# Mean squares of x by TensorE from the turned x, and bias rows on 64 partitions, in one step of a hybrid streaming encoder

## The chip, the cores and the metric

One NeuronCore of a Trainium2 chip runs the whole program in one launch. The metric is the device time of one execution in microseconds (us); three runs of the kernel before took 1779.07, 1780.92 and 1783.11 us, and their median is 1780.92 us. All data is float32. The engines are TensorE (PE), VectorE (DVE), ScalarE (ACT), GpSimd (POOL) and SyncE (SP), which issues the DMA transfers here.

## The reference

One layer of an encoder is computed for a prompt of 1024 rows and a sample of 64 rows; together they are 1088 rows of width 1024. What matters here is the first part, the normalised projection into queries, keys, values and forget logits:

```
def rms_norm(x, g):
    y = x * rsqrt(mean(x * x, axis=-1) + EPS)
    return y * g

h = rms_norm(x, g_norm1)
p = h @ w_in            # q_A k_A v_A | q_B k_B v_B | forget logits
```

Behind it come chunk-band attention with a learned relative-position bias (8 heads), forgetting attention (8 heads), an output projection, cross-attention into 256 memory tokens, and a feed-forward block with a causal convolution. The bias of the chunk-band attention depends on the distance of query and key alone: bias[i, j] = table[clip(i - j, -128, 128) + 128].

## The kernel before

The gain g_norm1 is multiplied into x ahead of the projection, and the factor rsqrt(mean + EPS) of each row is applied behind it. So the projection needs x turned (features on the partitions, rows along the free axis), and the mean square of each row has to be known when the products leave PSUM. The host hands over both forms: xT, turned, and xn, row by row.

The projection is done for eight pairs of heads, p = 0 to 7. Each pair goes through eight row tiles of 128 rows, t = 0 to 7, and one tile of the 64 sample rows. Pair 0 is also the stage in which x is loaded. Turned x comes in column chunks c = 0 to 4: chunks 0 to 3 hold 256 rows each, which are row tiles 2c and 2c + 1, and chunk 4 holds the samples. Each chunk is loaded in two halves z of four feature blocks k (load_x, line 163). split_x (line 126) makes two parts of each block: xhi on ACT (line 130; on POOL, line 128, for odd k of chunk 0) and the rest xlo on DVE (line 131). Each row tile's product (line 299) is then three matmuls for each of eight k, into a PSUM bank "pj".

The mean squares are done from xn: load_stats (line 144) loads 128 rows by 1024 into a tile "s", stats (line 149) squares them on ACT with a sum along the row into one column of ssq, and stats_end (line 156) adds EPS and forms rstd1 and eps1 with Ln, Exp and a refining step (rsq, line 72). proj (line 303) reads the product: ACT copies it (qkraw, line 309), squares it for the norm of queries and keys (line 233) and scales the values by rstd1 (line 312). Then norm does the norm of queries and keys on DVE and POOL, and turn transposes them on PE (line 326, bank "tq", of which there is one) and has ACT and DVE write kh, kl and q (lines 265 and 266). Scores (line 499), softmax (lines 502 to 509), transposes (line 539) and sums (line 554) of the attention are sub-steps too.

Order: weave (line 274) puts sub-steps between the pieces of three matmuls of a row tile's product. After piece number x + 1 of n, it issues sub-steps as long as the number issued times n is below the number of sub-steps times (x + 1); so the first sub-step comes right behind the first piece. early (line 591) says which loading work of pair 0 goes in front of (first list) or behind (second list) the other sub-steps of tile t. Row tiles 0 and 1 are done together, as 16 pieces that alternate between them. Everything is traced in this order; a scheduler may then change the order of an engine's instructions by when it thinks that they are ready. in_order (line 1822) keeps it from that: up to the end of t = 5 of pair 0, each instruction of PE, ACT, DVE and POOL is tied behind the one traced before it on its engine, and SP's up to load_rows(0) at the end of the opening. Later only a few kinds are tied.

The bias: load_rows (line 181) copies a head's row of the table, 769 long, to 128 rows in DRAM, and load_bias (line 445) reads them with a step of 768, which shifts each row by one (toeplitz, line 439); the lower 64 partitions read the copies 64 to 127. The samples' attention reads 64 such rows.

Of the kernel before, what the change touches and what calls it, by code (L numbers as in the profile page):

```python
# [7 lines left out]
F32 = mybir.dt.float32  # L8
F32R = mybir.dt.float32r
ACT = mybir.ActivationFunctionType  # L10
# [31 lines left out]
def hybrid_step(ctx: ExitStack, tc: tile.TileContext, i: dict, o: dict):  # L42
# [24 lines left out]
    sv = dram.tile([8, S, P], F32, name="sv")  # L67
    rows = dram.tile([8, P, 769], F32, name="rows")
    negc = dram.tile([8, T], F32, name="negc")
    negs = dram.tile([8, N], F32, name="negs")  # L70

    def rsq(pl, ms, out, n, rows=P):

        y = pl.tile([rows, n], F32, name="rsq_y", bufs=3)
        a = pl.tile([rows, n], F32, name="rsq_a", bufs=3)
        act.activation(y, ms, ACT.Ln)
# [8 lines left out]
    eps1 = small.tile([P, 9], F32, name="eps1")  # L85
    ssq = small.tile([P, 9], F32, name="ssq")
    flog = small.tile([P, 9, 8], F32, name="flog")
# [3 lines left out]
    dve.memset(flog, 0.0)  # L91
    dve.memset(ssq, 1.0)

# [47 lines left out]

    xns = {}

    def load_stats(t):
        rows = P if t < NT else S
        xn = xns[t] = wk.tile([P, N], F32, name="s", bufs=4)
        nc.sync.dma_start(xn[:rows, :D], i["xn"][t * P:t * P + rows])

    def stats(t):
        rows = P if t < NT else S  # L150
        if t not in xns:
            load_stats(t)
        xn = xns.pop(t)
        act.activation(xn[:rows, :D], xn[:rows, :D], ACT.Square, scale=1.0 / 32, accum_out=ssq[:rows, t:t + 1])

    def stats_end(t0, t1):
        ms = wk.tile([P, 9], F32, name="ms1", bufs=2)
        n = t1 - t0
        dve.tensor_scalar(ms[:, :n], ssq[:, t0:t1], EPS, None, op0=ALU.add)
        rsq(wk, ms[:, :n], rstd1[:, t0:t1], n)  # L160
        dve.tensor_scalar(eps1[:, t0:t1], ms[:, :n], EPS, None, op0=ALU.mult)

# [14 lines left out]
    def columns(c, z, raw=None):  # L177
        raw = raw or load_x(c, z)
        return [lambda k=k: split_col(c, k, raw) for k in range(4 * z, 4 * z + 4)]

    def load_rows(p):
        for head in range(2 * p, 2 * p + 2):
            nc.sync.dma_start(rows[head], i["table"][head:head + 1].broadcast_to([P, 769]))

# [26 lines left out]
    for d in range(2):  # L211
# [3 lines left out]
    xraws += [load_x(2, z) for z in range(2)]  # L215
    for t in (2, 3):
        load_stats(t)
    load_rows(0)
# [219 lines left out]

    def toeplitz(head, q, n, c=0):

        return bass.AP(rows.tensor, rows.offset + head * P * 769 + 128 + 769 * c, [[768, q], [1, n]])

    bias = {}

    def load_bias(p):
        for h in range(2):
            if p < 4:
                t = wa.tile([P, T], F32, name="bias", bufs=2)[:, :640]
                head = 2 * p + h
                dve.memset(t[0:64, 576:640], NEG)  # L450
                dve.memset(t[64:128, 0:64], NEG)
                nc.sync.dma_start(t[0:64, 0:576], toeplitz(head, 64, 576))
# [131 lines left out]

    def norms(*ts):
        return [lambda t=t: stats(t) for t in ts] + [lambda: stats_end(ts[0], ts[-1] + 1)]
# [138 lines left out]
    class Sample:  # L725
# [8 lines left out]
        def load(self):  # L734
# [6 lines left out]
            for h in range(2):  # L741
                r = slice(h * S, h * S + S)
                if p < 4:
                    nc.sync.dma_start(b[r, :n], toeplitz(2 * p + h, S, n))
                else:
                    nc.sync.dma_start(b[r, :n], negs[2 * (p - 4) + h:2 * (p - 4) + h + 1].broadcast_to([S, n]))
# [1173 lines left out]
```

## Time and profile before

| | before |
|---|---|
| median of three runs | 1780.92 us (1779.07 to 1783.11) |
| profiled execution, its span (the page has no other time of it) | 1782.6 us |
| PE busy | 1717.3 us, 96% of the span |
| DVE, ACT, POOL busy | 1217.0, 943.4, 646.1 us |
| mean granted clock of TensorE | 0.989 |
| moved by DMA | 199.88 MB, mean 112 GB/s |
| PE busy in the first 50 us | 38.29 us, clock 0.86, DMA engines 0.76 busy |
| row copies "s<-in_xn_dram" | eight of 512 KB, one of 256 KB, all in the first 75 us |

A line of the order of time reads: start in us from the begin of the span, duration in us, engine, line of the code, operation, tile written and tiles read, shapes, number; in brackets the idle time of the engine ahead of it, and who ended it. For a group "x4" the duration runs from the first start to the last end. Matmuls overlap, so the step from one start to the next is what one costs.

### The profile page before, as it was taken

The numbers are of one execution on the slowest core, as the hardware profiler recorded it, in microseconds if no ns is written. First come the engines' busy times: TensorE is split into PE (matmuls) and PEld (weight loads), VectorE is DVE, ScalarE is ACT, GpSimd is POOL, SyncE is SP. The second block draws the span as 40 slices with busy tenths as digits, with TensorE's granted clock in tenths as the row PEclk, the third lists the DMA queues.
The fourth block names the chain that finished last, engine by engine and source line by source line (L and its number), as shares of the span: only waits on it lengthen the run. The fifth ranks groups of instructions, "written<-read, shape, count | busy, mean of one in ns | idle before, by whom it ended". The sixth has DMA issues, their size and how long they took to land.

```text
span 1782.6 us, 34013 instructions
## 1 busy us (share of the span) xinstructions
PE 1717.3 (96%) x12432; PEld 1668.7 (94%) x12432; DVE 1217.0 (68%) x2659; ACT 943.4 (53%) x2074; POOL 646.1 (36%) x931
## 2 busy tenths in 40 slices
PE   7898999999998898999999999999999999999999
PEld 6888999999997787999999999999999999999999
DVE  5768667677677687533444379877777777649986
ACT  6756667677677577434555456433333333434432
POOL 3656667878777443443443611100000000000000
PEclk8999999999999899999999999999999999999999
DMA  7322122122112577641111563222222222693332
GB/s 246 99 63 62 59 77 79 49 74 77 50 55 81 175 259 248 194 140 46 54 54 54 153 217 103 76 80 73 83 82 89 82 73 73 226 339 130 118 105 88
DMA packets 136696, 199.88 MB, mean 112 GB/s; under 512 B 21240, under 2 KB 77688, under 8 KB 136528
## 3 DMA queue, kind: packets, MB, share of 16 engines
q1 hardware_dynamic: 136528, 197.70, 35.1%
q8 instruction: 98, 1.61, 0.4%
q14 instruction: 70, 0.57, 0.1%
HBM read 155.35 MB, written 45.44 MB: 113 GB/s over the span
## 4 chain that ended last, share of the span: by engine, by line
PE 49%; DVE 2%; issue 1%; POOL 1%; ACT 1%; DMA 0%; SPq 0%; DVEq 0%; POOLq 0%; ACTq 0%
PE W L1475 25%; PE W L1799 13%; PE pj L948 7%; PE S L1218 1%; PE tq L1254 1%; PE O L1254 1%; PE W L948 1%; POOL lo L930 1%; PE PT L1241 0%; DMA f<-x2d 0%; PE O L1218 0%; POOL s L1233 0%; PE PT L1199 0%; DVE lo L930 0%; ACT hi L929 0%
## 5 line engine op out<-in xcount | busy, mean ns | idle before, releaser
L299 PE MATMUL pj<-whi,xhi 128*128 128x384 f32 (+1 forms) x512 | 195.9, 383 | 2.2 <-ACT xhi L130 1.9
L299 PE MATMUL pj<-wlo,xhi 128*128 128x384 f32 (+1 forms) x512 | 176.9, 346 | 4.5 <-POOL wlo L123 4.5
L299 PE MATMUL pj<-whi,xlo 128*128 128x384 f32 (+1 forms) x512 | 176.3, 345 | 0.6 <-DVE xlo L131 0.6
L1581 POOL COPY s<-gp 128x2 f32<-128x2 f32 x22 | 15.8, 719 | 335.9 <-DVE gp L1580 335.9
L1475 PE MATMUL W<-h,hi 128*128 128x272 f32 x704 | 134.4, 288 | 1.4 <-ACT qlo L1611 1.4
L504 ACT ACTIVATE s<-s,mx 128x640 f32<-128x640 f32 (+7 forms) x128 | 94.4, 737 | 77.8 <-DVE mx L502 77.0
L1799 PE MATMUL W<-f,hi 128*128 128x272 f32 x672 | 127.1, 287 | 0.0
L541 DVE TENSOR_TENSOR ptl<-PT,pth 128x512 fp32r<-128x512 f32 (+2 forms) x192 | 99.4, 522 | 38.8 <-ACT pth L540 36.5
L1475 PEld LDWEIGHTS W<-h,hi 128*128 128x128 f32 x704 | 110.8, 188 | 1.7 <-ACT qlo L1611 1.6
L540 ACT CAST pth<-PT 128x512 fp32r<-128x512 f32 (+2 forms) x192 | 84.8, 449 | 43.8 <-PE PT L539 41.9
L299 PEld LDWEIGHTS pj<-wlo,xhi 128*128 128x128 f32 x512 | 99.6, 194 | 6.2 <-POOL wlo L123 6.1
L1799 PEld LDWEIGHTS W<-f,hi 128*128 128x128 f32 x672 | 105.3, 188 | 0.0
L299 PEld LDWEIGHTS pj<-whi,xhi 128*128 128x128 f32 x512 | 99.4, 194 | 4.4 <-ACT xhi L130 2.4
L1475 PE MATMUL W<-h,lo 128*128 128x272 f32 x352 | 101.8, 289 | 0.0
L299 PEld LDWEIGHTS pj<-whi,xlo 128*128 128x128 f32 x512 | 98.1, 192 | 1.8 <-DVE xlo L131 1.6
L539 PE MATMUL PT<-ident,s 128*128 128x128 f32 x528 | 90.5, 278 | 7.7 <-DVE ptl L541 7.3
L1799 PE MATMUL W<-f,lo 128*128 128x272 f32 x336 | 96.7, 288 | 0.0
L1339 ACT CAST hi<-raw 128x512 fp32r<-128x512 f32 x68 | 42.2, 621 | 98.5 <-PE W L1475 58.7
L948 PE MATMUL pj<-a,hi 128*128 128x384 f32 (+1 forms) x352 | 89.1, 336 | 2.5 <-ACT hi L929 1.6
L499 PE MATMUL S<-kh,q 128*128 128x256 f32 (+1 forms) x304 | 77.5, 280 | 13.1 <-DVE mx L502 13.1
L507 POOL TENSOR_SCALAR s<-s,ssum 128x640 f32<-128x640 f32 (+6 forms) x96 | 70.7, 738 | 47.5 <-DVE ssum L505 36.7
L554 PE MATMUL O<-pth,v 128*128 128x256 f32 (+1 forms) x304 | 78.0, 281 | 8.4 <-ACT mhi L265 7.7
(552 smaller groups left out, 6049.5 us busy)
## 6 DMA issues: line engine op xcount, KB each, us to landing
raw<-in_w_down_dram SPq DMA_DIRECT2D x45, 256.0 KB, 2.9
wraw<-in_w_dram SPq DMA_DIRECT2D x56, 192.0 KB, 2.5
raw<-in_w_up_dram SPq DMA_DIRECT2D x41, 256.0 KB, 2.7
h<-ad SPq DMA_DIRECT2D x32, 272.0 KB, 5.2
mwraw<-in_w_mkv_dram SPq DMA_DIRECT2D x16, 512.0 KB, 6.2
raw<-in_w_mo_dram SPq DMA_DIRECT2D x32, 256.0 KB, 3.2
kvraw<-in_w_down_dram SPq DMA_DIRECT2D x32, 256.0 KB, 3.1
ad<-t SPq DMA_DIRECT2D x22, 272.0 KB, 2.1
```

The costliest lines, as they stand in the source:

```text
L299: pe.matmul(pj[:, :nw], x2[a][:, k, t * P:(t + 1) * P], wt[k][b][:, :nw], start=n == 0, stop=n == 3 * KT - 1)
L499: pe.matmul(sp[:, a:a + (k1 - k0) * P], q, kk[:, h, src], start=m == 0, stop=m == 1)
L504: act.activation(s[:, :n], s[:, :n], ACT.Exp, bias=mx, scale=-1.0, accum_out=sm)
L507: pool.tensor_scalar(s[:, :n], s[:, :n], sm, 1.0, op0=ALU.mult, op1=ALU.mult)
L539: pe.transpose(pt[:, b - ch[0]], self.s[j][:, (b - w0) * P:(b - w0 + 1) * P], ident)
L540: act.copy(hi[:, f:f + n, j], pt[:, f:f + n])
L541: dve.tensor_tensor(lo[:, f:f + n, j], pt[:, f:f + n], f32(hi[:, f:f + n, j]), op=ALU.subtract)
L554: pe.matmul(op[:, cols], groups[p, b // 2].v[:, b % 2, h].rearrange("p a d -> p (a d)"), pt[:, x, cols], start=b == self.full[0] and m == ...
L948: pe.matmul(out()[:, :cn], w[a][:, k % 4], x[b][k][:, c0:c0 + cn], start=k == 0 and (a, b) == SPLIT[0], stop=k == KT - 1 and (a, b) == SPL ...
L1339: act.copy(hi, t)
L1475: pe.matmul(w[:, z, :Q], a(p, j), rights[j][b][:, z * Q:z * Q + Q], start=fresh and begin and j == 0 and x == 0, stop=final and end and j ...
L1799: pe.matmul(ws[m][:, z, :Q], la[p][:, m * P:(m + 1) * P], ra[b][:, z * Q:z * Q + Q], start=first and y == 0 and what in opening, stop=fina ...
```

## The change

The row-by-row form of x is no longer loaded. In its place, once a half chunk of turned x has been split, ACT squares the raw half in place (square), and PE sums the squares over the features: for each row tile of the chunk, eight float32 matmuls with 128 squared columns as the stationary side and a tile "two" of two columns of ones as the moving side add up in PSUM (stats). stats then adds EPS and calls rsq for both row tiles of a chunk. The squares of a half stand behind its four splits; the sums of a chunk are one sub-step, at the place in early where the row Squares of these tiles stood, except that tiles 7 and 8 are no longer done together: the sums of chunk 3 (tiles 6 and 7) stand at the end of t = 5 and those of chunk 4 at the end of t = 6. In t = 2 the sums stand ahead of scale_gain instead of behind it. The raw tiles of chunks 1 and 2 share buffers with the attention's pth and ptl, those of the others with "s".

Apart from that, the copies of the bias rows in DRAM are 64 in place of 128 for each head, and both halves of the partitions read the same 64 copies.

```diff
-    rows = dram.tile([8, P, 769], F32, name="rows")
+    rows = dram.tile([8, S, 769], F32, name="rows")
...
-    def stats(t):
-        rows = P if t < NT else S
-        if t not in xns:
-            load_stats(t)
-        xn = xns.pop(t)
-        act.activation(xn[:rows, :D], xn[:rows, :D], ACT.Square, scale=1.0 / 32, accum_out=ssq[:rows, t:t + 1])
-
-    def stats_end(t0, t1):
-        ms = wk.tile([P, 9], F32, name="ms1", bufs=2)
-        n = t1 - t0
-        dve.tensor_scalar(ms[:, :n], ssq[:, t0:t1], EPS, None, op0=ALU.add)
-        rsq(wk, ms[:, :n], rstd1[:, t0:t1], n)
-        dve.tensor_scalar(eps1[:, t0:t1], ms[:, :n], EPS, None, op0=ALU.mult)
+    sums = {}
+
+    def square(c, z, raw):
+        sums[c, z] = raw
+        act.activation(raw, raw, ACT.Square, scale=1.0 / 32)
+
+    def stats(c):
+
+        n, rows = (2, P) if c < 4 else (1, S)
+        st = bank("PT")[:, :4].rearrange("p (t z) -> p t z", z=2)
+        for z in range(2):
+            sq = sums.pop((c, z))
+            for k in range(4):
+                for t in range(n):
+                    pe.matmul(st[:rows, t], sq[:, k, t * rows:t * rows + rows], two, start=z + k + t == 0,
+                              stop=z == 1 and k == 3 and t == n - 1, skip_group_check=True)
+        ms = wk.tile([P, 2], F32, name="ms1", bufs=2)
+        if rows < P:
+            dve.memset(ms, 1.0)
+        dve.tensor_scalar(ms[:rows, :n], st[:rows, :n, 0], EPS, None, op0=ALU.add)
+        rsq(wk, ms[:, :n], rstd1[:, 2 * c:2 * c + n], n)
+        dve.tensor_scalar(eps1[:, 2 * c:2 * c + n], ms[:, :n], EPS, None, op0=ALU.mult)
...
-        return [lambda k=k: split_col(c, k, raw) for k in range(4 * z, 4 * z + 4)]
+        return [lambda k=k: split_col(c, k, raw) for k in range(4 * z, 4 * z + 4)] + [lambda: square(c, z, raw)]
...
-            nc.sync.dma_start(rows[head], i["table"][head:head + 1].broadcast_to([P, 769]))
+            nc.sync.dma_start(rows[head], i["table"][head:head + 1].broadcast_to([S, 769]))
...
-    for t in range(2):
-        load_stats(t)
     xraws += [load_x(1, z) for z in range(2)]
     wt = []
     for k in range(KT):
         wt.append(split_w(0, k, wraws[k]))
         split_col(0, k, xraws[k // 4])
+    for z in range(2):
+        square(0, z, xraws[z])
...
-    for t in (2, 3):
-        load_stats(t)
...
-                nc.sync.dma_start(t[64:128, 64:640], toeplitz(head, 64, 576, 64))
+                nc.sync.dma_start(t[64:128, 64:640], toeplitz(head, 576))
...
-    early = {1: lambda: (norms(0, 1) + columns(1, 0, xraws[2]), []),
-             2: lambda: (columns(1, 1, xraws[3]), [scale_gain] + norms(2, 3) + columns(2, 0, xraws[4]) + [lambda: load_bias(0)]),
-             3: lambda: (columns(2, 1, xraws[5]), norms(4, 5)), 4: lambda: ([], columns(3, 0)), 5: lambda: ([], columns(3, 1) + norms(6)),
-             6: lambda: ([], norms(7, 8) + columns(4, 0) + columns(4, 1))}
+    early = {1: lambda: (norms(0) + columns(1, 0, xraws[2]), []),
+             2: lambda: (columns(1, 1, xraws[3]), norms(1) + [scale_gain] + columns(2, 0, xraws[4]) + [lambda: load_bias(0)]),
+             3: lambda: (columns(2, 1, xraws[5]), norms(2)), 4: lambda: ([], columns(3, 0)), 5: lambda: ([], columns(3, 1) + norms(3)),
+             6: lambda: ([], columns(4, 0) + columns(4, 1) + norms(4))}
```

More of the change, by code (lines that the diff above doesn't have):

```diff
@@ L85, in hybrid_step @@
     eps1 = small.tile([P, 9], F32, name="eps1")
-    ssq = small.tile([P, 9], F32, name="ssq")
+    two = small.tile([P, 2], F32, name="two")
     flog = small.tile([P, 9, 8], F32, name="flog")
@@ L91, in hybrid_step @@
     dve.memset(flog, 0.0)
-    dve.memset(ssq, 1.0)
+    dve.memset(two, 1.0)
     right = ExitStack()
@@ L437, in forget, with toeplitz @@
         return [[logs]] + [[lambda a=a: turned(a)] for a in (0, 4, 8)] + [[lambda: scan(T)], [lambda: back(T), lambda: scan(N)], [lambda: back(N)]]
-    def toeplitz(head, q, n, c=0):
-        return bass.AP(rows.tensor, rows.offset + head * P * 769 + 128 + 769 * c, [[768, q], [1, n]])
+    def toeplitz(head, n):
+        return bass.AP(rows.tensor, rows.offset + head * S * 769 + 128, [[768, S], [1, n]])
     bias = {}
@@ L451, in load_bias @@
                 dve.memset(t[64:128, 0:64], NEG)
-                nc.sync.dma_start(t[0:64, 0:576], toeplitz(head, 64, 576))
-                nc.sync.dma_start(t[64:128, 64:640], toeplitz(head, 64, 576, 64))
+                nc.sync.dma_start(t[0:64, 0:576], toeplitz(head, 576))
+                nc.sync.dma_start(t[64:128, 64:640], toeplitz(head, 576))
             else:
@@ L583, in substeps, with norms @@
         return [f for f in r if f]
-    def norms(*ts):
-        return [lambda t=t: stats(t) for t in ts] + [lambda: stats_end(ts[0], ts[-1] + 1)]
     def scale_gain():
         dve.tensor_scalar(gd[:, :, 0], gd[:, :, 0], 0.125, None, op0=ALU.mult)
-    early = {1: lambda: (norms(0, 1) + columns(1, 0, xraws[2]), []),
-             2: lambda: (columns(1, 1, xraws[3]), [scale_gain] + norms(2, 3) + columns(2, 0, xraws[4]) + [lambda: load_bias(0)]),
-             3: lambda: (columns(2, 1, xraws[5]), norms(4, 5)), 4: lambda: ([], columns(3, 0)), 5: lambda: ([], columns(3, 1) + norms(6)),
-             6: lambda: ([], norms(7, 8) + columns(4, 0) + columns(4, 1))}
+    def norms(c):
+        return [lambda: stats(c)]
+    early = {1: lambda: (norms(0) + columns(1, 0, xraws[2]), []),
+             2: lambda: (columns(1, 1, xraws[3]), norms(1) + [scale_gain] + columns(2, 0, xraws[4]) + [lambda: load_bias(0)]),
+             3: lambda: (columns(2, 1, xraws[5]), norms(2)), 4: lambda: ([], columns(3, 0)), 5: lambda: ([], columns(3, 1) + norms(3)),
+             6: lambda: ([], columns(4, 0) + columns(4, 1) + norms(4))}
     forgetting = []
@@ L743, in load @@
                 if p < 4:
-                    nc.sync.dma_start(b[r, :n], toeplitz(2 * p + h, S, n))
+                    nc.sync.dma_start(b[r, :n], toeplitz(2 * p + h, n))
                 else:
```

5 lines of the change are left out of this document (removed).

## The prediction

> **What bounds the kernel now.** I read the shares of the engines first, then TensorE's busy time by stretches, then the order of single instructions in the first 60 us, where the change lies.
>
> ```profile
> span 1782.6 us, 34013 instructions
> PE 1717.3 (96%) x12432; PEld 1668.7 (94%) x12432; DVE 1217.0 (68%) x2659; ACT 943.4 (53%) x2074; POOL 646.1 (36%) x931
> ```
>
> The stretches below give length, TensorE's busy time (instructions), granted clock, share of the DMA engines and GB/s.
>
> ```profile
> 0.00:50.00 50.00, 38.29 (x173) 0.86 0.76 239
> ...
> 200.00:250.00 50.00, 48.94 (x345) 1.00 0.23 64
> ...
> 1200.00:1400.00 200.00, 200.00 (x1599) 1.00 0.24 79
> ```
>
> Nearly everywhere TensorE (PE) is the bound: what starts late in the first stage ends late, since there is no slack behind it. The first stage itself is different: 38.29 of 50 us busy at a clock of 0.86. There PE waits for others, and it waits in the order of the program:
>
> ```profile
> 28.12 0.66 PE L326 MATMUL tq<-ident,qk 128*128 128x128 f32 x4 [0.64 <-POOL qk L246]
> ...
> 33.44 0.63 PE L326 MATMUL tq<-ident,qk 128*128 128x128 f32 x4 [2.50 <-DVE q L266]
> ...
> 37.27 0.55 PE L499 MATMUL S<-kh,q 128*128 128x256 f32 x1 [2.44 <-DVE mx L502]
> ```
>
> At 28.12, 33.44 and 37.27 PE stands before a transpose or a score although projection products (L299) that need none of that come next in the code. in_order pins that order on PE, ACT, DVE and POOL up to the end of t=5 of pair 0. So in this stage it decides what each new instruction is put in front of.
>
> **The change part by part.** *Price of a mean-square matmul.* The changed kernel does 72 new float32 matmuls with two moving columns (16 for each of four chunks, 8 for the samples). L1199 is the same shape and type:
>
> ```profile
> 825.45 0.34 PE L948 MATMUL pj<-hhi,lo 128*128 128x384 f32 x1
> 825.62 0.72 PE L1199 MATMUL PT<-ones,sq 128*128 128x2 f32 x6
> 826.21 0.42 PE L948 MATMUL pj<-hhi,hi 128*128 128x384 f32 x1
> ```
>
> Six of them move the next product from 825.62 to 826.21: 0.59 us, 0.10 us each; 16 are 1.6 us, all 72 are 7 us. At the half clock of the early stretches a product's step grows from 0.18 us (22.69 to 22.87 below) to 0.33 us (21.22 to 21.55), so 16 take up to 2.9 us. [...]
>
> *The opening, the largest term.* In the weave of t=1 the first sub-step is issued behind the first of 16 pieces. Before, that was an ACT Square. Now it is stats(0): 16 matmuls on PE, behind three products and ahead of the other 45 of row tiles 0 and 1. They read the squares of both halves of chunk 0, and each Square overwrites its raw tile, so it waits until DVE has read the last of its four columns.
>
> ```profile
> 6.08 0.45 PE L299 MATMUL pj<-whi,xlo 128*128 128x392 f32 x1
> ...
> 13.47 0.45 PE L299 MATMUL pj<-whi,xhi 128*128 128x392 f32 x1 [1.90 <-ACT xhi L130]
> ```
>
> ```profile
> 21.22 0.53 PE L299 MATMUL pj<-wlo,xhi 128*128 128x392 f32 x1
> 21.55 0.53 PE L299 MATMUL pj<-whi,xlo 128*128 128x392 f32 x1
> 22.36 0.49 PE L299 MATMUL pj<-whi,xhi 128*128 128x392 f32 x1 [0.29 <-DVE flog L314]
> 22.69 0.34 PE L299 MATMUL pj<-wlo,xhi 128*128 128x392 f32 x1
> 22.87 0.34 PE L299 MATMUL pj<-whi,xlo 128*128 128x392 f32 x1
> ```
>
> ```profile
> 14.97 1.05 ACT L154 ACTIVATE s<-s 128x1024 f32<-128x1024 f32 x1
> ...
> 17.45 0.47 DVE L131 SCALAR_TENSOR_TENSOR xlo<-s,gcol,xhi 128x256 fp32r<-128x256 f32 x1
> ```
>
> The last xlo of chunk 0 ends at 17.92. The second Square (1.05 us, as at 14.97) then ends at about 19.05. PE, which now does 24 products before 11.6 and the rest from 13.47 on, stands from 6.5 to 16.1 (first Square, 14.97 + 1.05 and its signal), does 8 small matmuls, stands again to 19.1, does 8 more (1.5 us at half clock): 20.6. Then 45 products are left. I take half clock until 22.47, where it now ends: 6 products. The other 39 at 0.18 us end at 29.6; now the last ends at 22.08. **Opening: +7.5 us.** The bounds: all at full clock, 19.1 + 0.8 + 45 x 0.178 = 27.9, then 0.3 for the last: +6.2; half clock to 25.9, one step of 3.4 us longer: +9. The granted clock shows the loss to be feared:
>
> ```profile
> 5.00:10.00 5.00, 4.74 (x23) 1.00 0.99 317
> 10.00:15.00 5.00, 2.84 (x13) 1.00 1.05 395
> 15.00:20.00 5.00, 4.40 (x16) 0.56 0.93 234
> ```
>
> An idle of 1.9 us within 10 to 15 us is followed by a clock of 0.56. [...]
>
> *t=2 to t=4: the Squares in ACT's queue.* I keep the clock times of before, counted from the end of the opening.
>
> ```profile
> 22.91 1.71 ACT L130 ACTIVATE xhi<-ptl,gcol 128x256 fp32r<-128x256 f32 x4
> ...
> 28.13 0.20 ACT L76 ACTIVATE rsq_y<-ms 128x2 f32<-128x2 f32 x1 [0.95 <-DVE ms L159]
> ...
> 30.07 0.35 ACT L309 COPY qkraw<-pj 128x256 f32<-128x256 f32 x1
> ...
> 31.21 0.48 ACT L265 ACTIVATE q<-tq,gd 128x256 fp32r<-128x256 f32 x1
> ...
> 34.11 0.47 ACT L265 ACTIVATE kh<-tq,gd 128x256 fp32r<-128x256 f32 x1 [0.84 <-PE tq L326]
> ...
> 40.09 1.04 ACT L154 ACTIVATE s<-s 128x1024 f32<-128x1024 f32 x1
> ...
> 41.81 0.35 ACT L309 COPY qkraw<-pj 128x256 f32<-128x256 f32 x1
> ...
> 47.88 1.71 ACT L130 ACTIVATE xhi<-s,gcol 128x256 fp32r<-128x256 f32 x4
> ```
>
> ```profile
> 23.46 1.68 DVE L131 SCALAR_TENSOR_TENSOR xlo<-ptl,gcol,xhi 128x256 fp32r<-128x256 f32 x4 [0.17 <-DMA s<-in_xn_dram]
> ...
> 29.15 2.45 DVE L131 SCALAR_TENSOR_TENSOR xlo<-pth,gcol,xhi 128x256 fp32r<-128x256 f32 x4
> ...
> 33.33 1.67 DVE L131 SCALAR_TENSOR_TENSOR xlo<-ptl,gcol,xhi 128x256 fp32r<-128x256 f32 x4
> ...
> 36.83 0.29 DVE L502 CUSTOM_DVE_ANT_0 s<-S,bias 128x128 f32<-128x128 f32 x1
> ...
> 48.42 1.88 DVE L131 SCALAR_TENSOR_TENSOR xlo<-s,gcol,xhi 128x256 fp32r<-128x256 f32 x4
> ```
>
> t=2: the Square of chunk 1's second half runs 25.2 to 26.25 (xlo ends at 25.14), stats(1) on PE to 27.9, and Ln goes at 28.35 in place of 28.13: +0.2, since two row Squares leave the same place. PE loses 1.6 us here, under the 0.64 and 2.50 us that it now waits at 28.12 and 33.44; without them it would show.
>
> Still t=2: the Square of chunk 2's first half waits for xlo (29.15 + 2.45 + 0.2 = 31.8) and ends at 32.9. Behind it on ACT stand qkraw of tile 2 and kh, q of tile 0: q ends at 34.5, now 31.7. DVE's kl and q follow, and PE's transpose now at 33.44 goes at 35.7. t=3: the next xlo end at 37.3, that Square at 38.35, and only then comes kh of tile 1, now at 34.11; the score on DVE now at 36.83 comes at 40.3. **+3.45 us** at PE's scores (37.27).
>
> At the end of t=3 two row Squares (to 41.13) go away and stats(2) comes: six products at half clock and 16 small matmuls after 41.3 end at 46.2, and qkraw follows Ln and Exp at 46.7 in place of 41.81. **Total +4.9**; at full clock 2 less.
>
> t=4: chunk 3's first Square waits for xlo (50.3), ends at 51.4, and holds qkraw of tile 4, which now follows xhi at 49.5: **+1.9**.
>
> *t=5 and t=6.*
>
> ```profile
> 60.84 1.06 ACT L154 ACTIVATE s<-s 128x1024 f32<-128x1024 f32 x1 [1.62 <-DMA s<-in_xn_dram]
> ```
>
> Here ACT waits for a row copy, 1.62 us, with kh of tile 4 behind it. The column Square would end about 0.9 us earlier; stats(3) and stats(4) put 2.4 us on PE, and the last small Squares take about 2 us from ACT. I take 0. If stats(3) keeps its place while its Square is waited for, PE stands some 4 us: +3.9; if ACT's relief is kept, -2.
>
> *Loads.* Eight row copies and a half one leave, and the eight copies of the bias rows in DRAM halve:
>
> ```profile
> s<-in_xn_dram SPq DMA_DIRECT2D x8, 512.0 KB, 5.5
> ```
>
> SP issues the first of them behind what the opening waits for:
>
> ```profile
> 12.49 0.52 ACT L121 CAST whi<-bias 128x392 fp32r<-128x392 f32 x1 [3.79 <-DMA bias<-in_w_dram]
> ...
> 17.08 0.19 ACT L154 ACTIVATION_READ_ACCUMULATOR s<-s 128x1 f32 x1
> ```
>
> The weights of k=4..7 are ahead of the row copies on SP, and 1 MB of chunk 1 moves up into the freed place; the bias tiles are there before the score at 36.83. I put 0 to -0.5 us on it. The halved rows, the Toeplitz reads from row 0 for both halves, the removed accumulator reads (0.2 us each) and the memsets are hidden behind the waits above: 0. If that cover is gone, the reads alone are 9 x 0.2 = 1.8 us less on ACT.
>
> **Sum**: 7.5 + 4.9 + 1.9 + 0 = +14.3 us. The profiled span of 1782.6 becomes 1797; it is 1.7 us (0.1%) over the median of the runs, 1780.92, so the runs should show about 1795. The bounds: 6.2 + 2.9 + 0.5 - 2 - 0.5 = +7 and 9 + 5.3 + 1.9 + 3.9 = +20: 1788 to 1801.
>
> **Rivals.** *The small matmuls don't hold the opening* (PE gets round them, or the Squares come early). Then only their own 1.6 to 2.9 us a chunk are paid, and half of that falls into waits: +2 to +7, about 1785. For it: PE has 11.7 us of idle in the first 50. Against it: the waits at 28.12 and 33.44, which PE did not get round.
>
> *The loads decide, and it is faster.* Place: ACT's wait of 3.79 us for the weights at 12.49. If the 1 MB of row copies shares the DMA engines with them (0.99 to 1.05 busy there), its going frees up to 3.8 us, and the 1.62 us at 60.84 go too: -5, about 1776. It decides only from the point where stats(0) no longer stands ahead of the products; as long as PE stands to 19.1, earlier weights only bring the xlo chain forward, and the gain is set against +7.5. Against it as well: the weights were issued first.
>
> *The clock stays low.* If small matmuls don't count as work for the granted clock, all 45 products run at 0.33 us (+7 on the opening) and later stretches too: +22 to +30, about 1806. For it: the clock of 0.56 after an idle much shorter. Against: from 22.36 on the products are at 0.34 us again after some 6 us.
>
> **How the numbers follow.** Forecast 0.63; not held 0.14; loads 0.10; low clock 0.08; no change that can be told 0.05 (the 11.7 us of idle in the first 50 take up the whole opening, against which stands that those waits follow PE's own late results). About 0.2%, 3.6 us, is what a measurement of this kernel can tell from no change. Slower: 0.63 + 0.08 + two thirds of 0.14 = 0.80; faster 0.10; same 0.10. The range is 1784 to 1803: the forecast's own 1788 to 1801, and most of the first rival and the edge of the third.
>
> **What would show it.** In the changed profile: PE's first L299 products end near 6.5 us, the first two-column matmuls start near 16 and 19, and row tiles 0 and 1 end near 29 to 31, with a clock of about half from 12 to 22 us. ACT's Squares begin when DVE's xlo end, and qkraw stands behind them at t=2 and t=4. PE's busy time rises by about 7 us or less, its share of the first 50 us falls, and everything after 100 us looks as before, some 14 us later. I am wrong if the products of tiles 0 and 1 end before 25 us, or if the gap between the two kernels goes on changing behind t=6.

## The result, and the profile after

The changed kernel takes 1808.56 us (median of four runs, 1806.94 to 1810.63) beside 1781.05 us before (1779.07 to 1783.11). The ratio is 1.0159, 95% interval 1.0147 to 1.0171: 27.5 us slower. The prediction said slower, 1795 us, with a range up to 1803. So the sign was right and the size about half.

The page of the changed kernel begins:

```profile
span 1808.1 us, 34269 instructions
...
PE 1739.4 (96%) x12576; PEld 1692.9 (94%) x12576; DVE 1213.9 (67%) x2660; ACT 943.0 (52%) x2066; POOL 645.1 (36%) x931
```

PE has 144 instructions more than before (12432) and is busy for 22.1 us more. The change adds 72 matmuls. So twice as many new instructions stand in the trace as there are new matmuls in the code, and PE's busy time rose by three times the 7 us that the prediction allowed.

The stretches that the prediction showed of before, in the changed kernel (length, then busy time of PE, PEld, DVE, ACT and POOL with their instructions, granted clock, DMA share, GB/s; the clock is a share of TensorE's full speed, and in before a projection product's step is 0.18 us at 1.00 and 0.33 us at 0.50):

```profile
0.00:50.00 50.00, 36.74 (x187) 35.37 (x187) 21.70 (x62) 24.13 (x52) 15.42 (x25) 0.79 0.50 151
5.00:10.00 5.00, 1.17 (x8) 0.85 (x6) 2.94 (x6) 1.90 (x5) 2.38 (x3) 0.87 1.01 324
10.00:15.00 5.00, 0.61 (x3) 0.61 (x4) 3.40 (x5) 3.53 (x7) 3.60 (x4) 0.50 1.11 348
15.00:20.00 5.00, 5.00 (x25) 5.00 (x25) 1.19 (x3) 1.06 (x1) 0.04 (x1) 0.50 0.95 313
...
200.00:250.00 50.00, 50.00 (x347) 48.90 (x346) 32.54 (x99) 32.17 (x89) 31.71 (x46) 1.00 0.21 57
1200.00:1400.00 200.00, 200.00 (x1595) 200.00 (x1595) 152.94 (x260) 79.49 (x115) 18.23 (x40) 1.00 0.23 73
```

The late stretches look as before: full clock and no slack. The loss is made in the first stage. From 5 to 15 us PE is now busy 1.78 us of 10, in place of 7.58, and the clock is 0.50 from 10 to 20 us.

PE's row of the opening and of t=2 and t=3, in order of time (a group of small matmuls has the number of its instructions behind the x):

```profile
14.39 6.99 PE L156 MATMUL PT<-two,s 128*128 128x2 f32 x32 [8.22 <-ACT s L146]
...
21.24 0.67 PE L299 MATMUL pj<-whi,xhi 128*128 128x392 f32 x1
...
31.23 0.34 PE L299 MATMUL pj<-whi,xlo 128*128 128x392 f32 x1
```

```profile
34.53 1.84 PE L156 MATMUL PT<-two,pth 128*128 128x2 f32 x16
36.23 1.93 PE L156 MATMUL PT<-two,ptl 128*128 128x2 f32 x16
52.35 3.41 PE L156 MATMUL PT<-two,pth 128*128 128x2 f32 x16
55.62 3.55 PE L156 MATMUL PT<-two,ptl 128*128 128x2 f32 x16
```

PE stands 8.22 us for ACT's Square, as the prediction described. Then chunk 0's sixteen matmuls are 32 instructions and hold PE from 14.39 to 21.24: 6.85 us, where the prediction had 1.5 for the second half of them. Eight matmuls take 1.70 us at full clock (34.53 to 36.23, 0.21 each) and 3.27 us at half clock (52.35 to 55.62, 0.41 each). Tiles 0 and 1 end at 31.57 in place of 22.08.

ACT's Squares of columns and what stands behind them, and DVE's score:

```profile
13.29 1.05 ACT L146 ACTIVATE s<-s 128x1024 f32<-128x1024 f32 x1
...
16.28 1.06 ACT L146 ACTIVATE s<-s 128x1024 f32<-128x1024 f32 x1 [1.94 <-DVE xlo L131]
...
42.16 1.06 ACT L146 ACTIVATE pth<-pth 128x1024 f32<-128x1024 f32 x1 [1.73 <-DVE xlo L131]
...
59.40 0.20 ACT L76 ACTIVATE rsq_y<-ms 128x2 f32<-128x2 f32 x1 [6.72 <-DVE ms L161]
...
59.74 0.35 ACT L309 COPY qkraw<-pj 128x256 f32<-128x256 f32 x1
...
68.97 1.06 ACT L146 ACTIVATE s<-s 128x1024 f32<-128x1024 f32 x1 [0.74 <-DVE xlo L131]
69.94 0.35 ACT L309 COPY qkraw<-pj 128x256 f32<-128x256 f32 x1
```

```profile
50.36 0.29 DVE L502 CUSTOM_DVE_ANT_0 s<-S,bias 128x128 f32<-128x128 f32 x1
```

From these rows and those of before, the lateness can be followed through the first stage: 9.5 us at the end of tiles 0 and 1; 13.5 us at this score (36.83 before); 17.9 at qkraw of tile 3 (59.74 in place of 41.81); 20.45 at qkraw of tile 4 (69.94 in place of 49.49). The sample tile's copy out of PSUM comes 27.7 us late. The first two rows are of before, the third of the changed kernel:

```profile
49.49 0.35 ACT L309 COPY qkraw<-pj 128x256 f32<-128x256 f32 x1
...
83.95 0.48 ACT L351 COPY sm<-pj 64x392 f32<-64x392 f32 x1
```

```profile
111.68 0.48 ACT L351 COPY sm<-pj 64x392 f32<-64x392 f32 x1
```

From there the gap stays between some 24 and 28 us to the end (25.5 between the two profiled executions).

### The profile page after: what moved, and what is told of

Read it like the earlier page. It is cut to its first block, busy times and chain, and to the rows that moved or that the text cites. A ratio compares the mean times of both kernels' runs of the same rounds, so it can differ in the third digit from the quotient of the medians.

```text
span 1808.1 us, 34269 instructions
## 1 busy us (share of the span) xinstructions
PE 1739.4 (96%) x12576; PEld 1692.9 (94%) x12576; DVE 1213.9 (67%) x2660; ACT 943.0 (52%) x2066; POOL 645.1 (36%) x931
## 4 chain that ended last, share of the span: by engine, by line
PE 48%; DVE 2%; issue 1%; POOL 1%; ACT 1%; DMA 1%; DVEq 0%; POOLq 0%; ACTq 0%
PE W L1475 25%; PE W L1799 13%; PE pj L948 7%; PE S L1218 1%; PE tq L1254 1%; PE O L1254 1%; POOL lo L930 1%; PE PT L1241 0%; DVE lo L930 0%; PE O L1218 0%; DMA f<-x2d 0%; PE PT L1199 0%; POOL s L1233 0%; DVE qhi L1327 0%; ACT hi L929 0%
## 5 line engine op out<-in xcount | busy, mean ns | idle before, releaser
L499 PE MATMUL S<-kh,q 128*128 128x256 f32 (+1 forms) x304 | 78.1, 281 | 13.7 <-DVE mx L502 13.6
```

The costliest lines, as they stand in the source:

```text
L499: pe.matmul(sp[:, a:a + (k1 - k0) * P], q, kk[:, h, src], start=m == 0, stop=m == 1)
```

## The experiments

**Undoing one part at a time.** Three kernels give some chunks their row copies and row Squares back and keep column sums for the others; a fourth is the kernel before with only the 64 bias rows. The list of sums in early is cut accordingly (shown without the calls that return an empty list, and without the functions that come back from the kernel before):

```diff
 h0  (chunk 0 by row copies)
-    early = {1: lambda: (norms(0) + columns(1, 0, xraws[2]), []),
+    early = {1: lambda: (row_norms(0, 1) + columns(1, 0, xraws[2]), []),
 h12 (chunks 1 and 2 by row copies)
-             2: ... norms(1) + [scale_gain] + columns(2, 0, xraws[4]) + ...
+             2: ... [scale_gain] + row_norms(2, 3) + columns(2, 0, xraws[4]) + ...
-             3: lambda: (columns(2, 1, xraws[5]), norms(2)),
+             3: lambda: (columns(2, 1, xraws[5]), row_norms(4, 5)),
 h34 (chunks 3 and 4 by row copies)
-             5: ... columns(3, 1) + norms(3)),  6: ... columns(4, 0) + columns(4, 1) + norms(4))
+             5: ... columns(3, 1) + row_norms(6)),  6: ... row_norms(7, 8) + columns(4, 0) + columns(4, 1))
 rows (the kernel before, with)
-    rows = dram.tile([8, P, 769], F32, name="rows")
+    rows = dram.tile([8, S, 769], F32, name="rows")
...
```

> The changed kernel, with row tiles 0 and 1 taken back to row copies and row Squares on ACT; chunks 1 to 4 stay with the sums on TensorE. The theory of places (each chunk's sums cost where they stand, and the parts add up: 9.5 us in the opening, some 9 for chunks 1 and 2, some 9 for chunks 3 and 4) expects 9.5 us less than the changed kernel, about 1799. The rival that the opening governs all (what follows is late and at half clock only because the opening was) expects nearly all of the 27.5 us back, 1781 to 1786.

> The changed kernel, with row tiles 2 to 5 (chunks 1 and 2) taken back to row copies. The theory of places expects about 9 us less than the changed kernel, 1799.5. The rival that the opening governs expects 1806 to 1809, since the opening is untouched.

> The changed kernel, with row tiles 6, 7 and the samples (chunks 3 and 4) taken back to row copies. The theory of places expects about 9 us less than the changed kernel, 1799.5; if the prediction's term for t=5 and t=6 (nothing, with t=4's 1.9) were right, 1806.5. The rival that the opening governs expects 1806 to 1809.

> The kernel before with the second part of the change alone: 64 copies of each bias row in place of 128, and both halves of the partitions read them. Every theory of the sums expects 1781, within 2. The rival that this part carries some of the loss (both halves reading the same 64 rows of DRAM) expects 1784 or more.

Measured: h0 1802.17 us, ratio to before 1.0120 (1.0103 to 1.0137), so 6 us come back; h12 1797.67, 1.0099 (1.0084 to 1.0114), 11 us; h34 1800.40, 1.0115 (1.0100 to 1.0130), 8 us; rows 1780.88, 1.0007 (0.9998 to 1.0016). The bias rows do nothing that can be told. No part of the sums carries the whole loss: each of the three costs 6 to 11 us. The opening, which the prediction called the largest term, gives back no more than the others, and chunks 3 and 4, which it took at 0, cost about as much (the intervals of h0 and h34 overlap). That pointed to something that every chunk pays.

**Where the opening's sums stand, and what the Squares wait for.**

```diff
 late0
-    early = {1: lambda: (norms(0) + columns(1, 0, xraws[2]), []),
+    early = {1: lambda: (columns(1, 0, xraws[2]), norms(0)),
 own
-        sums[c, z] = raw
-        act.activation(raw, raw, ACT.Square, scale=1.0 / 32)
+        sq = raw
+        if c < 3:
+            sq = wk.tile([P, N], F32, name="s", bufs=4)[:, :1024].rearrange("p (k t) -> p k t", k=4)
+        sums[c, z] = sq
+        act.activation(sq, raw, ACT.Square, scale=1.0 / 32)
```

> The sums of chunk 0 are issued behind the weave's pieces of t=1 (columns(1,0)) in place of behind the first piece; all else as in the changed kernel. Theory (the opening's cost is PE standing before products that don't need the sums): the products of tiles 0 and 1 end near 22 again, the sums follow at 3.4 us or less, and the time falls by 4 to 6 us against the changed kernel, to about 1803. Rival (the place doesn't matter, since the row tiles' statistics are late either way and the next wait takes the gain): within 2 us of the changed kernel, about 1808. The first kernel with chunk 0 by row copies gave back 5.0, so this one should not give back more than that by much.

> The Squares of chunks 0 to 2 are written to tiles of their own in place of over the raw column tile, so that they need not wait until DVE has read the last column (xlo); the sums and their places stay. Theory (the waits of ACT for xlo of 1.94, 1.73 and 1.19 us lie on the path): the time falls by 3 to 5 us against the changed kernel, about 1804. Rival (the waits are for the raw tile's arrival or fall into PE's own lateness): within 2 us of the changed kernel, about 1808.

late0: 1802.13 us, ratio 1.0115 (1.0095 to 1.0136). About 6 us come back, as the theory had it: PE's stand in the opening costs 6 at the end, though tiles 0 and 1 were 9.5 late. own: 1808.53 us, ratio 1.0159 (1.0144 to 1.0174), not a bit less. Its Squares of chunk 0 run back to back, as the row of ACT shows, and the sums are as long as ever:

```profile
13.53 2.00 ACT L149 ACTIVATE s<-s 128x1024 f32<-128x1024 f32 x2
```

```profile
14.63 6.99 PE L159 MATMUL PT<-two,s 128*128 128x2 f32 x32 [7.72 <-ACT s L149]
...
35.49 4.68 PE L159 MATMUL PT<-two,s 128*128 128x2 f32 x32
```

ACT no longer waits for xlo ahead of a Square of chunks 0 to 2. So its waits of 1.94, 1.73 and 1.19 us in the changed kernel are not on the path that sets the end; the theory that they cost 3 to 5 us fell.

**The price of the matmuls.** ownpass is own with squares and ones of chunks 0 to 2 in fp32r, the type of xhi and xlo in the traces; the mean squares are then sums of squares in that type. pad is the kernel before, with its row copies and row Squares, and 72 two-column matmuls on the identity at the places of the sums; nobody reads their result.

```diff
 ownpass (on own)
-            sq = wk.tile([P, N], F32, name="s", bufs=4)[...]
+            sq = wk.tile([P, N], F32R, name="s", bufs=4)[...]
-            pe.matmul(st[:rows, t], sq[...], two, ...)
+            pe.matmul(st[:rows, t], sq[...], twor if c < 3 else two, ...)
 pad (on the kernel before)
+    def pad(n, rows):
+        def f():
...
+            for m in range(8 * n):
+                pe.matmul(st[:rows, m % n], ident[:, :rows], pads, start=m == 0, stop=m == 8 * n - 1, ...)
+        return [f]
-    early = {1: lambda: (norms(0, 1) + columns(1, 0, xraws[2]), []),
+    early = {1: lambda: (pad(2, P) + norms(0, 1) + columns(1, 0, xraws[2]), []),
...
```

> As the kernel with tiles of its own for the Squares, and squares and ones of chunks 0 to 2 in the rounded float32 type that the projections use (fp32r), so that a matmul of the sums should be one instruction in place of two: 48 instructions fewer on PE; the mean squares are then sums of rounded squares. Theory (the double instruction is the term that was mis-sized): 16 matmuls take half of 3.4 to 6.9 us, and the time falls by another 4 to 8 us, to about 1798. Rival (the count doesn't matter, the stand before the sums does): within 2 us of the kernel with tiles of its own, about 1804.

> The kernel before, with its row copies and row Squares, plus 72 float32 matmuls of two columns on the identity, whose result nobody reads, at the places where the changed kernel has its sums. They wait for nothing late. So this is the price of the matmuls alone. Theory of two instructions each: PE counts 144 instructions more, 0.21 us for each matmul at full clock, 15 us in all, of which the waits before transposes and scores hide some: +8 to +15 against the kernel before, 1789 to 1796. By the prediction's price (0.10 us each): +7 at most, less what the waits hide: 1783 to 1788. If the stand before the Squares is the whole cost, no change: about 1781.

ownpass: 1798.72 us, ratio 1.0103 (1.0087 to 1.0119), 9.8 us less than own. pad: 1794.43 us, ratio 1.0084 (1.0064 to 1.0105), 15 us slower than before with nothing waiting for a Square. In ownpass a chunk is 16 instructions:

```profile
14.77 3.58 PE L161 MATMUL PT<-twor,s 128*128 128x2 f32 x16 [8.04 <-ACT s L151]
...
31.87 1.86 PE L161 MATMUL PT<-twor,s 128*128 128x2 f32 x16
```

Half the instructions, half the time: 3.58 us beside 6.99 at half clock, and 1.86 beside 3.63 at full clock (late0's group, below). And L1199, from which the prediction took its price, shows the same doubling, once its group is counted against the code. Its line runs once for each row tile of each of 12 calls, 36 matmuls; the trace of before has 72. The first row is L1199 of before, the second and third are groups of the new line of the changed kernel:

```profile
L1199 PE MATMUL PT<-ones,sq x72: 165/251/251, 825.6 to 979.6; 128*128 128x2 f32 x64, 128*64 128x2 f32 x8
```

```profile
L156 PE MATMUL PT<-two,pth x32: 166/252/353, 34.5 to 55.4; 128*128 128x2 f32 x32
L156 PE MATMUL PT<-two,ptl x32: 251/302/353, 36.2 to 58.8; 128*128 128x2 f32 x32
```

(Each of the two halves of chunks 1 and 2 has eight matmuls, so 16 in all for pth, which stand as x32.) So "x6" at 825.62 were three matmuls, and their 0.59 us are 0.20 us for each, not 0.10.

**What two-column matmuls do to the clock.** pad's trace showed more than their own time. Its rows of PE, and PE's stretches (length, busy time, granted clock, DMA share, GB/s):

```profile
6.47 3.94 PE L150 MATMUL PT<-pads,ident 128*128 128x2 f32 x32
10.27 0.67 PE L311 MATMUL pj<-whi,xhi 128*128 128x392 f32 x1
```

```profile
6.00:9.00 3.00, 3.00 (x27) 1.00 0.90 284
10.00:16.00 6.00, 6.00 (x20) 0.50 1.06 387
24.00:27.00 3.00, 3.00 (x27) 0.95 0.71 265
28.00:33.00 5.00, 5.00 (x18) 0.50 0.83 258
```

PE has no idle time here at all: the small matmuls stand between full products. Yet the clock goes to 0.50 before each group has ended (at 9.62 and at 26.68 us, 3.2 and 2.4 us behind its start) and stays there for some 6 us of full products, whose step is then 0.33 us in place of 0.18: 18 products that cost 2.7 us more. In before, the fall at 15.64 us comes behind 1.50 us of idle; here the clock falls without an idle PE, so the busy share that the profile shows is not what it follows here. Three kernels ask whether it is the stretch of narrow work:

```diff
 padsplit (on pad): four pieces of 4 matmuls, spread over the turn's sub-steps
-            for m in range(8 * n):
+            for m in range(2 * n):
-        return [f]
+        return [f] * 4
 padwide (on pad): 29 wide products for a group of 16, 15 for the group of 8
-            for m in range(8 * n):
-                pe.matmul(st[:rows, m % n], ident[:, :rows], pads, ...)
+            last = 28 if n == 2 else 14
+            for m in range(last + 1):
+                pe.matmul(st[:, :256], x2[0][:, 0, :P], x2[0][:, 0, :256], ...)
 split (on late0): the sums of chunks 0 to 2 in two halves with other sub-steps between
-    early = {1: lambda: (columns(1, 0, xraws[2]), norms(0)),
+    early = {1: x[:4] + norms(0, 0) + x[4:] + norms(0, 1)   # x = columns(1, 0, xraws[2])
...
```

> The kernel with the padded matmuls, whose 16 per chunk are cut into four pieces of 4 (8 into four of 2), put between the other sub-steps of the same turn, so that products stand between them. The same 72 unread matmuls, 144 instructions. Theory of the clock (a stretch of two-column matmuls over 3 us long, though the profile counts PE as busy in it, is followed by some 6 us at half the granted clock): pieces of 0.85 us don't lower it; the stretches at 0.5 behind 9.6 and 27.3 us go, and the time falls by 3 to 9 us against 1794.4, to 1785 to 1791. Theory of the count alone (each matmul costs 0.21 us wherever it stands, the clock falls for other reasons): within 2 us of 1794.

> The kernel with the padded matmuls, where each group of 16 is replaced by 29 products of 256 columns in the projections' type on a column tile already there, unread too, and the group of 8 by 15. By the step of 0.178 us for 392 columns these take 0.116 us each, 3.4 us a group and 15 us in all, about the PE time of the two-column matmuls. Theory of the clock: wide products keep the clock at 1.00 where the two-column ones lowered it, and the time is 3 to 9 us less than 1794.4: 1785 to 1791. Rival (time on PE is what counts, whatever fills it): within 2 us of 1794.

> The kernel with late sums of chunk 0, whose sums of chunks 0 to 2 are issued in two halves of 8 matmuls (1.7 us at full clock), with other sub-steps and their products between. Theory of the clock: the stretches at 0.5 behind the sums of chunks 0 and 1 shrink or go, and the time falls by 3 to 7 us against 1802.1, to 1795 to 1799. Rival (the stands before scores and sums set the clock): within 2 us of 1802.

padwide: 1789.73 us, ratio 1.0048 (1.0033 to 1.0063), against 1.0084 for pad, whose interval begins where this one ends. About the same time on PE (3.48 us from 6.14 to the next product at 9.62, beside 3.80 in pad), and no drop of the clock:

```profile
6.14 3.64 PE L148 MATMUL PT<-xhi 128*128 128x256 f32 x29
```

```profile
10.00:16.00 6.00, 5.97 (x34) 1.00 1.06 386
24.00:27.00 3.00, 3.00 (x23) 1.00 0.74 277
28.00:30.00 2.00, 2.00 (x15) 1.00 0.87 230
```

padsplit: 1791.83 us, ratio 1.0058 (1.0041 to 1.0074). Both drops are gone as well, with the same 32 narrow instructions in each turn:

```profile
6.00:18.00 12.00, 12.00 (x75) 1.00 1.05 352
24.00:27.00 3.00, 3.00 (x24) 1.00 0.76 275
28.00:33.00 5.00, 5.00 (x40) 1.00 0.90 257
```

Its gain of 2.6 us on pad is less than the 3 that were the least expected, and the two intervals overlap, so the time alone decides nothing; later in its trace the clock falls in places where pad's didn't. The clock's rows decide it. split: 1795.07 us, ratio 1.0078 (1.0061 to 1.0094), 7 us less than late0. There the sums of chunk 1 were one group at half clock behind chunk 0's. Stretches of late0, then rows and stretches of split:

```profile
16.66 3.63 PE L156 MATMUL PT<-two,s 128*128 128x2 f32 x32
```

```profile
16.00:20.00 4.00, 4.00 (x36) 1.00 0.90 302
22.00:38.00 16.00, 15.74 (x59) 0.50 0.36 109
```

```profile
30.84 1.84 PE L160 MATMUL PT<-two,pth 128*128 128x2 f32 x16
34.77 1.84 PE L160 MATMUL PT<-two,ptl 128*128 128x2 f32 x16
```

```profile
16.00:28.00 12.00, 11.71 (x45) 0.50 0.79 237
30.00:44.00 14.00, 13.30 (x97) 1.00 0.00 1
```

In late0 the clock is half for 16 us behind chunk 0's sums, although PE is all but never idle, and the sums of chunk 1 fall in this stretch and cost double (eight matmuls take 3.26 us, 26.35 to 29.61, in place of 1.70). In split the pieces of 1.84 us, with products between, leave the clock at 1.00 from 30 to 44 us. It was not perfect: chunk 0's halves still stand in a low stretch from 16 to 28, with shorter idles ahead of it, and behind the second half of chunk 2 (45.91, with 1.75 us of idle shortly ahead) the clock falls again. The changed kernel itself holds both cases too: behind the one group of 34.53 to 38.16 the clock falls, and chunk 3's two groups of eight, 5 us apart, leave it alone.

```profile
40.00:42.00 2.00, 2.00 (x8) 0.50 0.01 4
...
80.00:90.00 10.00, 9.44 (x70) 0.98 0.16 41
```

The sixteen traces together tell more than these cases. In each of them the granted clock changes only on a grid of 3.41 us: before is at half clock for 6.83, 6.83, 3.41 and 3.41 us in its first 125, and pad's falls at 9.62, 26.68, 40.34, 47.16, 64.22 and 71.06 us lie 5, 4, 2, 5 and 2 steps of it apart. So the work can be counted for each step, called a window here, from the start and the shape of each PE instruction: how many moving columns the matmuls of a window have (392 for a projection product, 2 for each small instruction; a window full of products has some 7,500). In the first 125 us, counted from each trace's first record of the clock (at 5.40 us in before), there are 435 windows at full clock. All 51 with fewer than 2,700 columns are followed by half clock, all 375 with 2,950 or more by full clock; of the nine between, six by half. Idle time alone does not sort them so: windows without any idle fell (the changed kernel's from 35.96 us, with 2.06 us of small matmuls and 2,805 columns), and one with 1.77 us of idle did not (before's from 29.30 us). Among windows without idle, the 29 with 1.0 to 1.73 us of small matmuls stayed up, and the eight with 2.06 us or more fell. In these windows a stretch of small matmuls thus went with half clock much as idle time did. In whole windows at half clock, over these 125 us of one execution each: the changed kernel 13, before 6, rows 4, pad 9, padsplit 7, padwide 3, late0 12, split 9, lean 5.

**All of it together, and the opening filled.** lean has late sums in fp32r, as in ownpass, for chunks 0 to 2 and row copies for chunks 3 and 4. fill is the kernel before with the 64 bias rows and, in the opening, one group of 29 wide products that nobody reads; leanfill is lean with the same group.

```diff
 lean = ownpass + late0's order + h34's row copies
 fill, leanfill
+    def fill():
...
+        for m in range(29):
+            pe.matmul(st[:, :256], x2[0][:, 0, :P], x2[0][:, 0, :256], start=m == 0, stop=m == 28, ...)
-    early = {1: lambda: (norms(0, 1) + columns(1, 0, xraws[2]), []),
+    early = {1: lambda: ([fill] + norms(0, 1) + columns(1, 0, xraws[2]), []),
```

> Late sums of chunk 0, the sums of chunks 0 to 2 in one pass from tiles of their own, and chunks 3 and 4 by row copies again. If the parts found so far add up (6.0 for the late sums, 9.8 for one pass, 6.8 for chunks 3 and 4), 1808.5 - 22.6 = 1786. If they overlap, since each frees the same slack, 1788 to 1793. It leaves 48 matmuls of 0.11 us on PE, 5 us, so that it should not come below the kernel before, 1780.

> The kernel with the bias rows' part alone (row copies and row Squares as before), plus one group of 29 products of 256 columns at the start of t=1, unread. In the kernel with the padded wide products tiles 0 and 1 ended 2.6 us earlier than before, since the clock stayed at 1.00 where it now falls at 15.7. If the opening's half clock is what tiles 0 and 1 pay, and nothing behind takes the gain back, the time falls by 1.5 to 2.6 us, to about 1779. If the waits behind the opening take it back, it is the same as before, 1781, and then the first group's price in the padded kernels was nothing rather than a gain.

> The kernel with late one-pass sums for chunks 0 to 2 and row copies for chunks 3 and 4, plus the same group of 29 unread products. Its clock falls at 21.5 behind the first sums and stays low to 25. If filling the opening keeps it up, 1.5 to 2.6 us less than 1780.5: about 1778, below both kernels. If not, 1780 to 1782.

lean: 1780.47 us, ratio 0.9993 (0.9983 to 1.0003), lower than the sum of the parts (1786) and no different from before. A chunk's sums are now 1.84 us, and the one of chunk 1 leaves the clock up:

```profile
24.96 1.84 PE L185 MATMUL PT<-twor,s 128*128 128x2 f32 x16
```

```profile
24.00:34.00 10.00, 10.00 (x64) 0.98 0.31 88
```

fill: 1779.49 us, ratio 0.9993 (0.9984 to 1.0003). leanfill: 1779.63, 0.9996 (0.9986 to 1.0007). Filling the opening changes nothing that can be told, so the hope of a kernel below both was not met. A likely reason is in the kernel with the bias rows alone, which has no filling: in its profiled execution the clock of the opening stays up by itself, with less idle ahead.

```profile
10.00:15.00 5.00, 3.90 (x18) 1.00 1.05 396
15.00:20.00 5.00, 3.42 (x18) 1.00 1.10 321
```

The fall to 0.56 that the prediction read in the profile of before is thus not part of every execution.

## Why the prediction was right or wrong, point by point

*The price of a mean-square matmul: the step that failed.* "Six of them move the next product from 825.62 to 826.21: 0.59 us, 0.10 us each." They were six instructions of three matmuls. The true price is 0.21 us at full clock (34.53 to 36.23) and 0.41 at half (52.35 to 55.62), so 72 are 15 us and not 7. Counting L1199's executions in the code would have shown it before. The row held the whole price; the division was by instructions and not by matmuls. The trace of the changed kernel shows two instructions for each such matmul (144 for 72), and ownpass one instruction and half the time in fp32r (3.58 us for a chunk's 16, beside 6.99).

By the two profiles the sum of +14.3 us was short by 13: some 2 in the opening (9.5 for 7.5), 4 in t=2 to t=4 (11.0 for 6.8), and 7 in t=5 and t=6, which stood at 0.

*The clock.* The rival that small matmuls "don't count as work for the granted clock" had a chance of 0.08 and 1806 us, and was the nearest to 1808.56. Its mechanism is, in kind, what pad, padwide and split show: the eight windows of 3.41 us that had no idle and 2.06 us or more of narrow matmuls were all followed by half clock. That its amount came near is in part luck, since it reckoned with the price of 0.10 us and with half clock for all of the opening's 45 products, where some 13 had it (21.24 to 25.64). The argument against it, products at 0.34 us again "after some 6 us", held only for the time behind a stretch, and each chunk begins a new one.

*The opening, +7.5.* The order of events was right: PE stands from about 6 to 14.4 for the Squares, and the clock is low. That half clock follows the stand was an estimate from the one fall in before; the changed kernel has it from 8.65 to 25.72 us, close to the upper bound's 25.9, and that bound's step of 3.4 us is the grid of 3.41 us that the traces show. The stand was a little shorter (first small matmul at 14.39, predicted 16.1), the small matmuls much longer (6.85 us), and tiles 0 and 1 ended 9.5 late, at 31.57 beside "near 29 to 31". The 9.5 goes by the one profile of before; against that of rows, whose opening kept its clock, the lateness is 13.6 (31.57 for 18.00). But it is not carried to the end at its full size: late0 gives 6 back and h0 6, not 9.5. That the waits behind a late opening take up the rest is likely, not shown: the transposes' waits of 0.64 and 2.50 us are gone or 0.28 us in the changed kernel, but the score's of 2.44 us is 3.48.

*t=2 to t=4.* Predicted 3.45 us to the score, 4.9 by qkraw of tile 3, and 1.9 at tile 4, the first from Squares in ACT's queue ahead of qkraw. The lateness grew by 4.0 us to the score, 4.4 more to qkraw of tile 3, and 1.8 at tile 4 (20.45 less 18.65, by which PE's score ahead of it was late: 64.44 in place of 45.79). The first and the last fit in size, but the cause given for the first does not stand: own took the wait for xlo away and gained nothing. What fits is PE's own time, 3.5 us for the sums of chunk 1 (34.53 to 38.02), and for chunk 2 6.7 us with another low clock (52.35 to 59.03).

*t=5 and t=6, taken as 0: the term that was most short.* From 20.45 at qkraw of tile 4 to 27.7 at the sample tile: 7.3 us, beyond the bound of 3.9. h34 gives about 8 back at the end, and pad, where no sum waits for a Square, loses as much there (6.8 us late at the score of t=4, 15.0 at the sample tile's copy). This was called a cost that ACT's relief would offset. PE pays some 4.5 us for these sums at full clock (2.4 in the prediction), and no run shows such a relief on the path.

*Loads, bias rows, the late stages.* The bias rows do nothing, as predicted (rows 1.0007), and behind 120 us the gap is constant within a few us. The rival that the loads decide took ACT's wait of 3.79 us for the weights as the row copies' doing. That wait is 2.16 us in the changed kernel, at 10.80, but 2.06 us in rows too, at 10.90, where all row copies are still loaded: it was of that one execution of before.

*The account as the runs leave it.* Of the 27.5 us, about 15 come with the matmuls alone (pad): some 9 by their time on PE, since 15 us of wide products cost 9 (padwide), and some 6 by the clock, which is the difference of the two; since padwide has fewer windows at half clock (3) than before has (6, or 4 in rows), the 9 may be too low and the 6 too high. The other 12 come with what the sums wait for and when: 6 are PE's stand in the opening (late0). The last 6 are not shown one by one; split, which takes 7 off late0, got them from the clock and from the place of the halves together. The steps overlap, as the runs of the single parts (6, 11 and 8) also do, so each share is good to some 3 us.

## What to carry to other kernels

Before a row of the trace is divided by its count, set the count against the code: here 72 matmuls stood as 144 instructions. A run of narrow matmuls on TensorE cost twice in these kernels, once for its time (some 9 of pad's 15 us) and once for the clock behind it (some 6), though the profile shows the engine busy. The clock stayed at 1.00 with up to 1.73 us of them in a window of 3.41 us and wide products for the rest, so short runs are worth a try; in the type that was issued as one instruction they took half the time (3.58 us a chunk beside 6.99). And a reduction that ScalarE did beside a row copy was worth nothing to remove here, where TensorE is busy for 96% of the span: the best form with TensorE's sums that was run only equals the kernel before (lean, ratio 0.9993).

## What the runs showed of the hardware

- A float32 matmul with two moving columns stands in these traces as two instructions of 0.105 us, the same matmul in fp32r as one of 0.11 us (16 in 1.84 us, with the end of the last). At half clock both took about double: 0.41 us for the two instructions (52.35 to 55.62 in the changed kernel), 3.58 us for 16 in fp32r (ownpass, from 14.77).
- The granted clock fell to 0.50 although PE was busy without a gap, in every window of 3.41 us that held 2.06 us or more of two-column matmuls and otherwise full products (eight windows; behind the start of pad's second group and of own's the clock fell after 2.4 us each). It stayed at 1.00 with up to 1.73 us of them (29 windows), as with padsplit's pieces of 0.95 us. With idle beside them it fell behind less of them, as behind lean's first group of 1.84 us, with 0.57 us of idle in its window.
- What sorts these cases and the idle ones alike is the number of moving columns in a window: below 2,700 always half clock, from 2,950 on always full, in the first 125 us of the sixteen traces. Later in the executions there are a few exceptions (eight of the 100 windows below 2,700, two of some 8,000 from 2,950 on). That the hardware itself counts columns is not shown.
- Two profiled executions with the same code in the opening (before, and before with the bias rows) differ in whether the clock falls there at all: before has a window with 1.50 us of idle and 2,893 columns from 12.23 us on, and rows has none below 3,445 between 7 and 27 us. A single profile is not enough to put a price on such a fall.
